# RMSNorm and matmul on one core: the first eight output tiles in one store, two loads for every later group of x, smaller last stores

## The chip, the cores and the metric

The kernel runs on one core of a Trainium2 chip. The metric is the device time in microseconds of one execution. All other times below are from one profiled execution; they count from the first instruction of the program in the profile.

## The reference

`x` has 16 x 1024 tokens of 512 features in float32, `weight` is 512 x 768, `gamma` is a vector of 512, and the output is float32.

```python
batch, seq, dim, out_dim = 16, 1024, 512, 768
def reference(x, gamma, weight, eps):
    rms = np.sqrt(np.mean(x ** 2, axis=-1, keepdims=True) + eps)
    x_norm = x / rms * gamma
    return np.matmul(x_norm, weight).astype(np.float32)
```

So 33.6 MB of x and 1.6 MB of weights are read, and 50.3 MB are written.

## The kernel before

The 16384 tokens are cut into 128 tiles of 128 tokens, one token to a partition. Two tiles make a pair `j`, and the main loop runs over the pairs. For each tile VectorE or GpSimd prepare the operand, TensorE multiplies it with the bf16 weights (gamma is multiplied into them at the start), and the row factor 1/rms is applied when the product is evicted from PSUM.

The work of one tile is this. GpSimd casts x to bf16 (`cast`, L186, or `cast_quad`, L258). Of every 16 tiles 12 are transposed by TensorE (`transpose_word`, L228) and copied out of PSUM by VectorE (`evac`, L237); the other four are transposed by VectorE alone in 32x32 blocks (`move`, L269). ScalarE sums the squares (`square`, L194), some four pairs ahead of the matmuls, takes the root (L199), and VectorE inverts it (L201). TensorE does four steps of a 512 wide and a 256 wide matmul (`product`, L298) into one of three PSUM accumulators. The eviction (`finish_tile`, through `scale`) multiplies by 1/rms and writes the tile into an output buffer: ScalarE takes the even tiles (L277), VectorE the odd ones (L279).

The buffers are counted in tiles. x has two buffers `xt` of `XG` = 16 tiles; group g of x is in buffer g % 2. The output has three buffers `ot` of `OG` = 8 tiles; group g of the output is in buffer g % 3. The helper `stretches` says in which pieces a group is moved: for x a list for the first group, `[2, 2, 4, 8]`, two halves for some groups, and otherwise the whole group; for the output likewise.

All loads of x, all weights and all stores are issued by SyncE (SP), in the order in which the program recorded them, and lie on one DMA queue. `load(i)` (L175) issues one piece of x; `store(i)` (L291) issues a piece of the output when its last tile is evicted. The two first groups of x are issued at the start, before anything else needs SP. A later group is recorded by `load_until` in the last pair of the group before the one before it, and stands on SP behind the store that ends there. So SP's order in the steady part is store, store, load, store, store, load, and each store waits for its tiles.

`rows` maps tiles to rows of x and out in HBM. Tokens are dealt so that one partition has several neighbouring tokens: in a group of 16 tiles a partition has 16 neighbouring tokens, so that a load of the whole group reads 32 KB rows, a load of a half reads 16 KB rows that are 32 KB apart, and a store of eight tiles writes 24 KB rows. The first 16 tiles are dealt by pieces: the pieces of 2, 2, 4 and 8 tiles have 2, 2, 4 and 8 neighbouring tokens to a partition, and the pieces of the output there keep to the same borders.

`Order` records every operation with the cells that it reads and writes, and `emit` works out the waits. For each engine `known` holds how far it knows every other engine and every transfer to be; `needs` are the waits that remain, and `awaited` is their union. A transfer that nobody awaited is returned in `last`, and SP waits for all of them at the end of the kernel (L468 in the profile). The last tile of a store's piece also waits for the eviction of the tile before it (`before` in `finish_tile`), so that SP needs one wait only.

Of the kernel before, what the change touches and what calls it, by code (L numbers as in the profile page):

```python
# [20 lines left out]
class Order:  # L21
# [17 lines left out]
    def emit(self):  # L39
        nc = self.tc.nc  # L40
        streams = {id(e): n for n, e in enumerate((nc.tensor, nc.vector, nc.scalar, nc.gpsimd, nc.sync))}
        writer, readers = {}, {}
        known = [dict() for _ in streams]
        clocks, needs, place, slot_of, slots = [], [], [], {}, []
        count = [0] * len(streams)
        for n, (proc, engine, _, reads, writes) in enumerate(self.ops):
            at = streams[id(engine)]
            if proc is None:
                me, turn = ("transfer", n), 1
            else:  # L50
                count[at] += 1
                me, turn = at, count[at]
            written = {writer[cell] for cell in reads + writes if cell in writer}
            read = {d for cell in writes for d in readers.get(cell, ())}
            need = []
            for d in sorted(written | read, reverse=True):
                who, when = place[d]
                if who == me and (engine is nc.tensor or d not in written):
                    continue
                if known[at].get(who, 0) < when:  # L60
                    need.append(d)
                    for k, v in clocks[d].items():
                        known[at][k] = max(known[at].get(k, 0), v)
            if proc is None:
                free = [k for k, d in enumerate(slots) if known[at].get(("transfer", d), 0)]
                if free:
                    slots[free[0]] = n
                else:
                    slots.append(n)
                slot_of[n] = ("slot", slots.index(n))  # L70
            clock = dict(known[at])
            clock[me] = turn
            place.append((me, turn))
            clocks.append(clock)
            needs.append(need)
            for cell in reads:
                readers.setdefault(cell, []).append(n)
            for cell in writes:
                writer[cell], readers[cell] = n, []
        awaited = {d for need in needs for d in need}  # L80
        last = [n for n, (me, _) in enumerate(place) if not isinstance(me, int) and n not in awaited]
        sems, marks, done = {}, {}, {}
        for n in range(len(self.ops)):
            me = slot_of.get(n, place[n][0])
            if n in slot_of or n in awaited:
                if me not in sems:
                    sems[me] = self.tc.alloc_semaphore(f"done{len(sems)}")
                done[me] = done.get(me, 0) + (16 if n in slot_of else 1)
                marks[n] = (sems[me], done[me])
        for n, (proc, engine, issue, _, _) in enumerate(self.ops):  # L90
            for d in needs[n]:
                engine.wait_ge(*marks[d])  # L92
            ins = issue()
            if n in marks:
                ins.then_inc(marks[n][0], 16 if n in slot_of else 1)
        return [marks[n] for n in last]
# [3 lines left out]
def kernel(  # L100
# [18 lines left out]
    _, O = out.shape  # L119
    K = D // P  # L120
    NT = N // P
    NP = NT // 2
    XG, OG = 16, 8
    AHEAD = 20

    def stretches(group, parts):
        first, size, i = {}, {}, 0
        for g in range(NT // group):
            for n in parts.get(g, [group]):
                for t in range(i, i + n):  # L130
                    first[t], size[t] = i, n
                i += n
        return first, size

    last = NT // OG - 1
    x_first, x_size = stretches(XG, {0: [2, 2, 4, 8], **{g: [8, 8] for g in (1, 2, 5, 6, 7)}})
    o_first, o_size = stretches(OG, {0: [2, 2, 4], 1: [4, 4], last: [4, 4]})

    def rows(ap, i, n):
        base, t = (x_first[i], x_size[i]) if i < XG else (i - i % XG, XG)  # L140
        return ap[base * P:(base + t) * P, :].rearrange("(p t) d -> p t d", t=t)[:, i - base:i - base + n, :]

    def sb(name, shape, dtype):
# [29 lines left out]
    def load(i):  # L173
        dst, to = x_of(i, x_size[i])
        order.transfer(SP, lambda: SP.dma_start(out=dst, in_=rows(x, i, x_size[i])), writes=to)  # L175
# [110 lines left out]
    def store(i):  # L286
        first, n = o_first[i], o_size[i]
        s = first // OG % 3
        if i == first + n - 1:
            src = ot[s][:, first % OG:first % OG + n, :]  # L290
            order.transfer(SP, lambda: SP.dma_start(out=rows(out, first, n), in_=src), reads=cells("ot", s, first % OG, n))  # L291
# [181 lines left out]
```

## Time and profile before

| what | value |
|---|---|
| median of 6 executions | 209.92 us (209.60 to 210.28) |
| the profiled execution | 209.96 us |
| its span, first to last instruction | 208.0 us |
| TensorE busy, granted clock | 193.2 us (93%), 0.991 |
| VectorE, ScalarE, GpSimd busy | 149.4, 144.3, 59.9 us |
| data queue (SP): bytes, share of 16 DMA engines | 85.46 MB, 97.2% |
| stores | 20: 13 of 3072 KB, 5 of 1536 KB, 2 of 768 KB |
| loads of x | 16: 11 of 2048 KB, 2 of 4096 KB, 1 of 1024 KB, 2 of 512 KB |

The span is the time between the first and the last instruction; 1.96 us of the execution's own time lie around it. A busy share is an average over the whole span. In the tables of windows a line holds the window in us, its length, the busy time and the number of instructions of TensorE, its weight loads, VectorE, ScalarE and GpSimd, then the granted clock, the mean busy share of the 16 DMA engines, and their GB/s. A packet is counted in the window in which it starts, so a short window can show a little over 1. In lines of a timeline the first two numbers are start and duration, and what stands in brackets is the idle time before and what ended it.

### The profile page before, as it was taken

The page shows a single profiled execution, that of the slowest core. Times are in us where ns is not written, and L with a number is a line of the kernel's source. Part 1 is how long each engine was busy: PE and PEld are TensorE (multiplying, and loading weights), DVE is VectorE, ACT ScalarE, POOL GpSimd, SP SyncE. Part 2 cuts the span into 40 slices and gives each one's busy share as a digit, 9 for nine tenths or more (in the row PEclk, how much of TensorE's full clock was granted, in tenths as well). Part 3 has the DMA queues.
Part 4 walks back from the last instruction along what each step waited for, and adds up shares of the span by engine and source line. Part 5 has one row for each costly group of instructions (what it writes and reads, how often), then busy time and mean ns, then how long its engine had stood idle before and what let it go on. Part 6 is the DMA issues. An engine that isn't in the chain of part 4 may idle for free.

```text
span 208.0 us, 2760 instructions
## 1 busy us (share of the span) xinstructions
PE 193.2 (93%) x1212; PEld 72.7 (35%) x717; DVE 149.4 (72%) x255; ACT 144.3 (69%) x343; POOL 59.9 (29%) x34
## 2 busy tenths in 40 slices
PE   7889999999999999997999999999999999999920
PEld 1234444333334333432334333443334333443300
DVE  0455647998499957997469984999569984999510
ACT  4698897777768496754977687677877697663310
POOL 3247642036300390004900660006700174000000
PEclk9999999999999999999999999999999999999996
DMA  6999999999999999999999999999999999996995
GB/s 228 419 447 419 353 407 432 432 438 421 447 451 428 405 424 460 417 419 424 424 424 430 421 425 433 422 427 441 416 424 432 441 441 410 444 421 255 439 392 232
DMA packets 5488, 85.62 MB, mean 412 GB/s; under 512 B 610, under 2 KB 612, under 8 KB 1380
## 3 DMA queue, kind: packets, MB, share of 16 engines
q1 hardware_dynamic: 5472, 85.46, 97.2%
q8 instruction: 7, 0.11, 0.2%
q14 instruction: 5, 0.04, 0.0%
q10 hardware_dynamic: 4, 0.00, 0.0%
HBM read 35.13 MB, written 50.33 MB: 411 GB/s over the span
## 4 chain that ended last, share of the span: by engine, by line
PE 71%; DMA 16%; DVE 5%; issue 2%; SPq 1%; ACT 1%; POOL 1%; ACTq 0%
PE ps L298 62%; DMA xt<-in_x_dram 16%; PE ps L228 8%; DVE ot L279 2%; DVE xTq L269 2%; DVE xT L237 1%; POOL xb L186 1%; ACT jk L194 0%; SPq L343 0%; SPq L175 0%; ACT ot L277 0%; SPq L291 0%; DVE rstd L201 0%; SPq L468 0%; ACTq L92 0%
## 5 line engine op out<-in xcount | busy, mean ns | idle before, releaser
L298 PE MATMUL ps<-w_bf,xT 128*128 128x256 bf16 (+1 forms) x783 | 145.0, 325 | 3.0 <-ACT ot L277 1.3
L277 ACT ACTIVATE ot<-ps,rstd 128x768 f32<-128x768 f32 x64 | 57.5, 898 | 42.6 <-PE ps L298 41.0
L194 ACT ACTIVATE jk<-xt 128x512 bf16<-128x512 f32 x128 | 78.8, 618 | 8.2 <-DMA xt<-in_x_dram 8.2
L186 POOL CAST xb<-xt 128x2048 bf16<-128x2048 f32 (+3 forms) x21 | 46.4, 2221 | 113.1 <-DMA xt<-in_x_dram 111.8
L279 DVE TENSOR_SCALAR ot<-ps,rstd 128x768 f32<-128x768 f32 x64 | 64.8, 1013 | 9.9 <-PE ps L298 9.3
L294 PEld LDWEIGHTS <-xT 128*128 128x128 bf16 x400 | 39.3, 98 | 60.8 <-issue 52.9
L228 PE MATMUL ps<-ident_f,xb 128*128 128x128 f32 x200 | 54.4, 277 | 0.9 <-POOL xb L186 0.9
L237 DVE COPY xT<-ps 128x1024 bf16<-128x1024 bf16 (+1 forms) x53 | 34.5, 653 | 24.2 <-PE ps L228 22.5
L269 DVE STREAM_TRANSPOSE xTq<-xq 32x256 f32<-32x256 f32 x112 | 48.8, 435 | 3.4
L228 PEld LDWEIGHTS ps<-ident_f,xb 128*128 128x128 f32 x200 | 28.4, 143 | 46.4 <-issue 42.9
L298 PE MATMUL ps<-w_bf,xTq 128*128 128x256 bf16 (+1 forms) x217 | 41.8, 324 | 0.4
L194 ACT ACTIVATION_READ_ACCUMULATOR jk<-xt 128x1 f32 x128 | 24.3, 190 | 0.0
L294 PEld LDWEIGHTS <-xTq 128*128 128x128 bf16 x112 | 11.0, 98 | 14.5 <-issue 14.5
L258 POOL CAST xq<-xt 128x2048 bf16<-128x2048 f32 x7 | 13.3, 1897 | 0.0
L201 DVE RECIPROCAL rstd<-rms 128x8 f32<-128x8 f32 (+3 forms) x20 | 3.9, 193 | 8.1 <-ACT rms L199 7.8
L199 ACT ACTIVATE rms<-ssq,eps_sb 128x8 f32<-128x8 f32 (+3 forms) x20 | 6.0, 300 | 0.6
L298 PE MATMUL ps<-warm 128*128 128x512 bf16 x10 | 4.4, 583 | 1.4 <-DVE eps_sb L352 1.4
L277 ACT ACTIVATE w_bf<-w_f,g_sb 128x768 bf16<-128x768 f32 x2 | 1.9, 935 | 1.3 <-DMA w_f<-in_weight_dram 1.3
L375 DVE COPY g_sb<-ps 128x4 f32<-128x4 f32 x1 | 0.2, 160 | 3.2 <-PE ps L369 3.2
L339 ACT ACT_TABLE_LOAD x1 | 1.3, 1283 | 1.5 <-SPq L432 1.5
L279 DVE TENSOR_SCALAR w_bf<-w_f,g_sb 128x512 bf16<-128x512 f32 (+2 forms) x3 | 1.4, 481 | 0.7 <-DMA w_f<-in_weight_dram 0.7
L369 PEld LDWEIGHTS ps<-ident_f,g_row 2*128 2x128 f32 x2 | 0.3, 200 | 2.6 <-issue 2.6
(10 smaller groups left out, 2.0 us busy)
## 6 DMA issues: line engine op xcount, KB each, us to landing
out_dram<-ot SPq DMA_DIRECT2D x13, 3072.0 KB, 16.0
xt<-in_x_dram SPq DMA_DIRECT2D x11, 2048.0 KB, 20.5
xt<-in_x_dram SPq DMA_DIRECT2D x2, 4096.0 KB, 23.4
out_dram<-ot SPq DMA_DIRECT2D x5, 1536.0 KB, 11.3
w_f<-in_weight_dram SPq DMA_DIRECT2D x2, 768.0 KB, 5.6
out_dram<-ot SPq DMA_DIRECT2D x2, 768.0 KB, 16.1
xt<-in_x_dram SPq DMA_DIRECT2D x2, 512.0 KB, 5.2
xt<-in_x_dram SPq DMA_DIRECT2D x1, 1024.0 KB, 9.1
```

What stands on the lines that cost most here:

```text
L186: run(POOL, lambda: POOL.tensor_copy(out=xb[s][:, i % 8:i % 8 + n, :], in_=src), of, cells("xb", s, i % 8, n))
L194: run(ACT, lambda: ACT.activation(out=jk[j], in_=src[:, 0, :], func=AF.Square, accum_out=ssq[:, i:i + 1]), of, [("jk", j), ("ssq", i)])
L199: run(ACT, lambda: ACT.activation(out=rms[:, s], in_=ssq[:, s], func=AF.Sqrt, scale=1.0 / D, bias=eps_sb), [("ssq", t) for t in range(i, i ...
L201: run(DVE, lambda: DVE.reciprocal(out=rstd[:, s], in_=rms[:, s]), [("rms", i)], [("rstd", t) for t in range(i, i + n)])
L228: run(PE, lambda: PE.transpose(out=tp[b][:, t, h, :], in_=words[:, lo:lo + P], identity=ident_f), cells("xb", s, j % 4 * 2 + t) + ["ident" ...
L237: run(DVE, lambda: DVE.tensor_copy(out=dst[:, t:t + n, :], in_=src[:, t:t + n, :]), [("tp", b)], cells("xT", j % 4, t, n))
L258: run(POOL, lambda: POOL.tensor_copy(out=xq[s], in_=src), of, [("xq", s)])
L269: run(DVE, lambda: DVE.transpose(out=dst, in_=src), [("xq", s)], [("xTq", s)])
L277: run(ACT, lambda: ACT.mul(out=dst, in_=src, mul=r), reads, writes)
L279: run(DVE, lambda: DVE.tensor_single_scalar(out=dst, in_=src, scalar=r, op=mybir.AluOpType.mult), reads, writes)
L294: run(PE, lambda: PE.ldweights(lhsT), [cell])
L298: run(PE, lambda: PE.add_instruction(mybir.InstMatmult(name=nc.get_next_instruction_name(), engine=mybir.EngineType.PE, ins=[PE.lower_ap(r ...
```

## The change

There are three edits of how the work is cut, and one in the list of final waits.

- Tiles 0 to 15 are dealt by eight tokens to a partition throughout. The loads of tiles 0-1, 2-3 and 4-7 keep their sizes, and read 4, 4 and 8 KB of every 16 KB in HBM. Output group 0 has no entry any more, so its eight tiles are stored together.
- Every group of x from 1 on is loaded in two halves; before, groups 3 and 4 were loaded whole.
- Output group 14 (tiles 112 to 119) is stored in halves, and the last group (tiles 120 to 127) in pieces of 4, 2 and 2 tiles instead of 4 and 4.
- `last` in `emit` is chosen by `known` instead of by `awaited`.

```diff
         awaited = {d for need in needs for d in need}
-        last = [n for n, (me, _) in enumerate(place) if not isinstance(me, int) and n not in awaited]
+        seen = {who for clock in known for who in clock}
+        last = [n for n, (me, _) in enumerate(place) if me not in seen and not isinstance(me, int)]
...
-    x_first, x_size = stretches(XG, {0: [2, 2, 4, 8], **{g: [8, 8] for g in (1, 2, 5, 6, 7)}})
-    o_first, o_size = stretches(OG, {0: [2, 2, 4], 1: [4, 4], last: [4, 4]})
+    x_first, x_size = stretches(XG, {0: [2, 2, 4, 8], **{g: [8, 8] for g in range(1, NT // XG)}})
+    o_first, o_size = stretches(OG, {1: [4, 4], last - 1: [4, 4], last: [4, 2, 2]})
 
     def rows(ap, i, n):
-        base, t = (x_first[i], x_size[i]) if i < XG else (i - i % XG, XG)
+        base, t = (i - i % 8, 8) if i < XG else (i - i % XG, XG)
         return ap[base * P:(base + t) * P, :].rearrange("(p t) d -> p t d", t=t)[:, i - base:i - base + n, :]
```

The order of the instructions of TensorE, VectorE, ScalarE and GpSimd stays as it is. SP has two stores fewer at the start, one load more in each of groups 3 and 4, and one store more in each of the last two output groups.

## The prediction

> **What bounds the kernel now.** I read the page first, then the DMA windows around the end, then the one stall of TensorE, then the DMA windows of the start. Two things are full at once.
>
> ```profile
> PE 193.2 (93%) x1212; PEld 72.7 (35%) x717; DVE 149.4 (72%) x255; ACT 144.3 (69%) x343; POOL 59.9 (29%) x34
> q1 hardware_dynamic: 5472, 85.46, 97.2%
> out_dram<-ot SPq DMA_DIRECT2D x1, 1536.0 KB, 6.6
> ```
>
> TensorE is busy 93% of the span, and the one data queue keeps 16 DMA engines busy 97.2% of it: 202.2 us of 208.0, with 85.46 MB. The third line is the DMA view of the last 9 us: the last store is issued at 199.98 and lands 6.6 us later, at 206.6; the span ends 1.4 us after that. Whoever stops here says: the last store is too big and too late. The windows before it say something else (window, its length, busy time of each engine, granted clock, DMA share, GB/s):
>
> ```profile
> 185.21:186.12 0.91, 0.91 (x8) 0.38 (x4) 0.88 (x4) 0.20 (x1) 0.00 (x0) 1.00 1.00 432
> 186.12:187.04 0.92, 0.92 (x8) 0.32 (x4) 0.90 (x1) 0.03 (x1) 0.00 (x0) 1.00 0.87 374
> 187.04:187.95 0.91, 0.86 (x7) 0.46 (x5) 0.87 (x2) 0.88 (x1) 0.00 (x0) 1.00 0.63 270
> 187.95:188.86 0.91, 0.91 (x8) 0.24 (x3) 0.84 (x3) 0.00 (x0) 0.00 (x0) 1.00 0.44 189
> 188.86:189.77 0.91, 0.91 (x7) 0.29 (x3) 0.88 (x2) 0.00 (x0) 0.00 (x0) 1.00 0.32 135
> 189.77:190.68 0.91, 0.91 (x8) 0.29 (x3) 0.87 (x2) 0.85 (x1) 0.00 (x0) 1.00 0.19 81
> 190.68:191.60 0.92, 0.92 (x8) 0.29 (x3) 0.86 (x2) 0.06 (x1) 0.00 (x0) 1.00 1.00 427
> ```
>
> The queue runs dry because tiles 112 to 119 are stored only at 190.23. But it does not run dry at once: the share falls step by step to 0.19, which is 3 of 16 engines, and those 3 are still at work on the old store when the new one arrives. So 13 engines idle, on average over all 16 by 0.13x0.92 + 0.37x0.91 + 0.56x0.91 + 0.68x0.91 + 0.81x0.91 = 2.33 us, and the slowest three by nothing. A transfer has landed when its last engine is done: the store issued at 177.70 lands at 192.0 (14.3 us later), some 5 us after the first engines were through. From 190.68 to the end no engine stops, and all finish together. The slowest engine is thus busy from the first load to the last store; that chain, not TensorE, sets the end.
>
> TensorE has one stall, on the load of group 4 (tiles 64 to 79), issued whole at 72.01 and landed at 96.3:
>
> ```profile
> 96.38 0.63 ACT L194 ACTIVATE jk<-xt 128x512 bf16<-128x512 f32 x1 [3.63 <-DMA xt<-in_x_dram]
> 98.55 1.46 PE L298 MATMUL ps<-w_bf,xT 128*128 128x512 bf16 x8 [1.32 <-ACT ot L277]
> ```
>
> ScalarE waits 3.63 us for the data, its eviction of tile 56 stands behind that in order, and TensorE loses 1.32 us. Last, the start:
>
> ```profile
> 22.00:24.00 2.00, 1.95 (x15) 0.84 (x9) 1.70 (x3) 1.30 (x6) 2.00 (x1) 1.00 1.12 442
> 24.00:26.00 2.00, 2.00 (x15) 0.71 (x7) 1.05 (x2) 2.00 (x6) 1.45 (x1) 1.00 0.90 213
> 26.00:28.00 2.00, 2.00 (x15) 0.82 (x9) 0.58 (x2) 2.00 (x6) 0.00 (x0) 1.00 0.96 370
> 28.00:30.00 2.00, 2.00 (x15) 0.86 (x9) 1.60 (x2) 2.00 (x7) 1.01 (x1) 1.00 0.99 413
> ```
>
> The engines stay occupied here, yet from 24 to 28 they move (427-213)x2 + (427-370)x2 = 542 KB less than at the 427 GB/s of other stretches: 1.27 us lost by all engines alike, cause not visible.
>
> **The change, part by part.** The sum is made along the slowest DMA engine, in its order of transfers, against the profiled execution: span 208.0, 1.96 around it, 209.96, which is 0.04 above the median of 209.92.
>
> *Tiles 0 to 7 in one store.* Three stores (issued 13.00, 16.51, 23.88) become one at 23.88. The early two bought nothing: the second lands 16.1 us after its issue, at 32.6, because the loads of tiles 8 to 31, 6.3 MB, were queued ahead of it and the engines are on them until about 27. The merged store is there before that, so no gap: 0. If the loads drained early, the cover would be 27 - 23.9, about 3 us. SP's later issues keep their times. Row sizes change the pace a little: 6 KB rows ran at 413 GB/s (28 to 30 us), 12 KB rows at 427 (32 to 36), 24 KB rows at 432 (184.3 to 186.1). Half of 3.146 MB at 413 and half at 427 is 7.49 us, all at 432 is 7.28: -0.21.
>
> *The first four loads, rows by eight tokens.* The loads of tiles 0-1, 2-3 and 4-7 keep rows of 4, 4 and 8 KB, now spaced 16 KB apart in HBM instead of dense. No row shows this spacing. Nearest are the 16 KB rows spaced 32 KB: 425 to 429 GB/s (40 to 46, 110.3 to 114 us) against 430 for dense 32 KB rows. Below: 0, nothing here gains from sparser rows. Above: all 2.10 MB at the worst pace seen, 213 instead of 427, is +4.9. I take 0, as the near row has the same half-skipped pattern at full pace. The Trainium skill speaks against this edit: "DMA: Bandwidth & Descriptors", Latency and other measured facts, lists copies that slow down where rows are pitched at large powers of two. Its smallest listed pitch, 512 KiB, ran at 207 GB/s beside 214 for a padded one; by that ratio, an estimate, the three loads would cost 0.2 us more, and by the trace nothing.
>
> *Groups 3 and 4 in two loads each.* Same bytes, order and issue point; one more issue on SP each (about 0.95 us), after a store and with over 9 us until SP's next: 0. Tiles 64-71 land about 2.097 MB/430 = 4.9 us before the whole, near 91.4, so the stall of 1.32 goes. TensorE then runs 1.3 us ahead. Next late are the first half of group 7 (issued 143.77, landed 165.3; by the 22.9 us that the stalled load could have taken, and 1.3 earlier, wanted at 165.4) and output buffer 2 (stored at 154.29, free at 177.5, wanted then too): both just in time. Pace: 8.389 MB at 427 instead of 430.5: +0.16. What the 1.3 us are worth at the end: nothing, since the slowest DMA engine was not waiting for TensorE.
>
> *Tiles 112-119 in two stores.* The first goes about 6 us before 190.23, while the queue is still full, so the 2.33 us of mean idle go. The slowest three had none: 0. Pace 427 for 432 on 3.146 MB: +0.09. *Last group 4, 2, 2:* the last tile is evicted near 198.6 instead of 199.95; alone, its 0.786 MB would be down by about 198.6 + 0.3 + 1.9 + 1.4, near 202, but the slowest engine still has its backlog. Pace 413 for 427 on 1.573 MB: +0.13. The skill's rule in the same page, Measured, asks for at least 1 MiB in a DMA and promises only 75% of peak from there; for these two stores, an estimate at 75% of 427, that would be 1.2 us instead of 0.13. The 6 KB rows at 413 decide. New waits of DVE on ScalarE's eviction of the tile before (tiles 115, 125) are met about a tile time earlier: 0.
>
> *"Fewer waits at the end".* A transfer enters `known` only where some engine needs it, and there it enters `awaited` too: both tests pick the same transfers. What changes is the cut of the stores: groups 13, 14, 15 leave 1+2+3 = 6 waits instead of 1+1+2 = 4. No row shows a met wait alone. Below, 0; above, the 1.4 us from the last landing to the end hold four of them and the closing barrier, so 0.35 each, 0.7. I take 0.05, because the older transfers have landed before SP looks.
>
> Sum: -0.21 + 0.16 + 0.09 + 0.13 + 0.05 = +0.22; 209.96 + 0.22 = 210.18, less 0.04: **210.1 us**. About 0.2% (0.42 us) is what can be told from no change here, so this is no change. Its own range is 209.6 to 210.7, for the engines' lags may fall a little differently.
>
> **The rivals.** *The slow stretch at 24 to 28 goes* with the transfers around it: -1.27, 208.9. For: it begins as the store at 23.88 is issued, and nothing like it with all engines comes again. Against: it hits loads that the change leaves alone, and the issues at 13.00 and 16.51 did nothing of the kind.
>
> *The end follows the mean, not the slowest engine:* if the lag of the three engines comes anew in each stretch, or they catch up when others have finished, the 2.33 us are won: 209.96 - 2.33 + 0.22, about 207.8. For: the window of 0.19, TensorE's freed 1.32. Against: three engines without any idle.
>
> *Slower: the spaced first rows.* All DMA engines carry them first, and the slowest has no slack to make it up, so each lost microsecond is one at the end. At half pace for the 1.05 MB with 4 KB of every 16 KB it is 1.05/0.213 - 1.05/0.427 = 2.5; half of that gives 211.3. It decides once tiles 4-7, landed at 11.93, come over 0.5 us later.
>
> *It doesn't do what it says:* true of the waits, and in the sum.
>
> **How the numbers follow.** No change 0.50 (in its range 0.08 faster, 0.30 same, 0.12 slower); slow stretch gone 0.16; mean engine 0.13; spaced rows 0.21. Faster 0.08 + 0.16 + 0.13 = 0.37, same 0.30, slower 0.12 + 0.21 = 0.33. The range, 208.4 to 211.4, leaves out the mean-engine case and the upper third of the spaced rows, 0.20.
>
> **What would show it.** Right: no TensorE stall at 96 to 99, DMA share at 1.0 through 186 to 191, TensorE done near 197.6, and in exchange a share that slopes down over the last 4 us with the last landing still at 206 to 207. Wrong: a square end of the DMA share near 204 (mean engine); 427 GB/s through 24 to 28; a first load landing after 4.3 and the fourth after 12.4 (spaced rows).

## The result and the profile after

The changed kernel takes 210.48 us (median of 22 runs, 210.27 to 211.54) beside 210.04 us for the kernel before in the same series (45 runs): a ratio of 1.0025, 95% interval 1.0018 to 1.0032. By the ratio it is slower by 0.53 us (by the two medians 0.44), a little over the 0.2% from which the prediction would speak of a change; the interval begins just below that. The profiled execution took 210.45 us with a span of 208.4.

The three lines of the page and of the DMA view of the end, now of the changed kernel:

```profile
PE 192.7 (92%) x1212; PEld 72.3 (35%) x717; DVE 149.3 (72%) x255; ACT 144.7 (69%) x343; POOL 60.0 (29%) x34
q1 hardware_dynamic: 5760, 85.46, 97.3%
out_dram<-ot SPq DMA_DIRECT2D x1, 768.0 KB, 7.1
```

Bytes and busy time are what they were. The last store has half the size, is issued at 199.75 instead of 199.98, and takes 7.1 us to land instead of 6.6: 206.8 instead of 206.6. The windows before the end (same columns as before: window, length, five engines, granted clock, DMA share, GB/s):

```profile
187.04:187.95 0.91, 0.86 (x7) 0.30 (x3) 0.84 (x3) 0.65 (x1) 0.00 (x0) 1.00 1.00 432
187.95:188.86 0.91, 0.91 (x7) 0.29 (x3) 0.88 (x2) 0.00 (x0) 0.00 (x0) 1.00 0.95 405
188.86:189.77 0.91, 0.91 (x8) 0.29 (x3) 0.88 (x2) 0.16 (x1) 0.00 (x0) 1.00 0.95 405
189.77:190.68 0.91, 0.91 (x8) 0.28 (x3) 0.84 (x3) 0.74 (x1) 0.00 (x0) 1.00 1.01 432
...
203.00:204.00 1.00, 0.00 (x0) 0.00 (x0) 0.00 (x0) 0.00 (x0) 0.00 (x0) 0.50 0.68 283
204.00:205.00 1.00, 0.00 (x0) 0.00 (x0) 0.00 (x0) 0.00 (x0) 0.00 (x0) 0.50 0.40 166
205.00:206.00 1.00, 0.00 (x0) 0.00 (x0) 0.00 (x0) 0.00 (x0) 0.00 (x0) 0.50 0.15 61
206.00:207.00 1.00, 0.00 (x0) 0.00 (x0) 0.00 (x0) 0.00 (x0) 0.00 (x0) 0.50 0.02 6
```

The hole of 187 to 191 is filled, as the finer store of tiles 112 to 119 was to fill it. The idle time has not gone, it has moved: after 203 one engine after another has nothing left, and from 205 on 15% of them, two or three, work for the end. The same slope stood at 187 before.

The trace says the same in another way. It has sixteen landing signals for every transfer, as many as there are engines, and a transfer has landed with the last of them. In the kernel before, those of the store issued at 177.70 come from 187.37 to 191.98, and three of them (191.72, 191.80, 191.98) only after the next store is issued at 190.23: the three engines of the share of 0.19. In the changed kernel those of the last store come from 203.29 to 206.82.

TensorE's stall at 97 is gone as well. In the timeline of the changed kernel TensorE works from 94.75 to 100 without a wait; then ScalarE, two lines of a sum of squares and the eviction that comes after them:

```profile
94.75 5.04 PE L299 MATMUL ps<-w_bf,xT 128*128 128x512 bf16 x30
97.34 0.62 ACT L195 ACTIVATE jk<-xt 128x512 bf16<-128x512 f32 x1
97.86 0.19 ACT L195 ACTIVATION_READ_ACCUMULATOR jk<-xt 128x1 f32 x1
98.53 0.90 ACT L278 ACTIVATE ot<-ps,rstd 128x768 f32<-128x768 f32 x1 [0.48 <-PE ps L299]
```

Nothing here waits for a load; ScalarE waits for TensorE. But the last eviction starts at 198.71, only 0.22 us earlier than before, because the start is late (without the late start, below, it is 1.5 us earlier). These are the first sums of squares of the kernel before and of the changed one:

```profile
4.30 0.63 ACT L194 ACTIVATE jk<-xt 128x512 bf16<-128x512 f32 x1 [1.53 <-DMA xt<-in_x_dram]
```

```profile
5.62 0.63 ACT L195 ACTIVATE jk<-xt 128x512 bf16<-128x512 f32 x1 [2.86 <-DMA xt<-in_x_dram]
```

The first load, the same 0.52 MB, is 1.32 us later. And the stretch of slow transfers has another place. First the kernel before, then the changed kernel, then its later windows:

```profile
24.00:28.00 4.00, 4.00 (x29) 1.52 (x16) 1.63 (x3) 4.00 (x11) 1.45 (x1) 1.00 0.93 291
```

```profile
24.00:28.00 4.00, 4.00 (x27) 1.57 (x16) 2.81 (x5) 3.30 (x10) 2.72 (x2) 1.00 1.02 428
...
44.00:48.00 4.00, 3.95 (x27) 1.62 (x16) 3.80 (x9) 3.08 (x9) 3.31 (x1) 1.00 1.04 336
```

At a share near 1 the engines are occupied and move a fifth to a third less: at 24 to 28 before, at 44 to 48 after (where the kernel before had 424 GB/s). The changed kernel also runs at 396 and 390 GB/s from 32 to 36 and 36 to 40.

One view would have misled here. The page's chain of waits gives 88% of the changed kernel's span to TensorE, where it gave 71% before. It is followed back from the last instruction, through the last eviction; the seven microseconds of the last store, and the queue that store stands in, are not what it counts.

### The profile page after: what moved, and what is told of

Read it like the earlier page. It is cut to its first block, busy times and chain, and to the rows that moved or that the text cites. A ratio compares the mean times of both kernels' runs of the same rounds, so it can differ in the third digit from the quotient of the medians.

```text
span 208.4 us, 2764 instructions
## 1 busy us (share of the span) xinstructions
PE 192.7 (92%) x1212; PEld 72.3 (35%) x717; DVE 149.3 (72%) x255; ACT 144.7 (69%) x343; POOL 60.0 (29%) x34
## 4 chain that ended last, share of the span: by engine, by line
PE 88%; DMA 5%; issue 1%; SPq 1%; POOL 1%; DVE 0%
PE ps L299 78%; PE ps L229 10%; DMA xt<-in_x_dram 5%; POOL xb L187 1%; DVE ot L280 0%; SPq L176 0%; SPq L344 0%; SPq L469 0%; SPq L433 0%
## 5 line engine op out<-in xcount | busy, mean ns | idle before, releaser
L299 PE MATMUL ps<-warm 128*128 128x512 bf16 x10 | 3.9, 530 | 1.4 <-DVE eps_sb L353 1.4
```

Source lines behind the costliest of these rows:

```text
L299: run(PE, lambda: PE.add_instruction(mybir.InstMatmult(name=nc.get_next_instruction_name(), engine=mybir.EngineType.PE, ins=[PE.lower_ap(r ...
```

## The experiments

Two theories ran through the prediction. By the first, the slowest DMA engine sets the end and TensorE's time does not matter; by its rival, the end follows TensorE or the mean of the engines. Medians below are beside the kernel before in the same series.

**The edits one by one.** First the halves and the finer last stores together, without the first edit:

```diff
-    x_first, x_size = stretches(XG, {0: [2, 2, 4, 8], **{g: [8, 8] for g in (1, 2, 5, 6, 7)}})
-    o_first, o_size = stretches(OG, {0: [2, 2, 4], 1: [4, 4], last: [4, 4]})
+    x_first, x_size = stretches(XG, {0: [2, 2, 4, 8], **{g: [8, 8] for g in range(1, NT // XG)}})
+    o_first, o_size = stretches(OG, {0: [2, 2, 4], 1: [4, 4], last - 1: [4, 4], last: [4, 2, 2]})
```

> The kernel before with the load halves and the finer last stores, but with tiles 0 to 7 dealt and stored as before. Slowest-engine theory (the end is the backlog of the slowest DMA engine): the first load lands at 4.3 as before, TensorE has no stall at 96 to 99 and its last eviction ends near 198.6, and still the time is 210.0 to 210.5, since only the pace terms (+0.16 +0.09 +0.13 +0.05) reach the end; the DMA share slopes down over the last 4 us. Mean-engine theory: 2.3 us are won, 207.6 to 208.0. If the late first load of the changed kernel is what made it slower, this one is at least 0.3 us faster than the changed kernel.

Measured: 210.17 beside 209.92, ratio 1.0012 (1.0001 to 1.0023). The last eviction ended at 198.4, 1.5 us before that of the kernel before, and the last store took 8.6 us to land. So 1.5 us of TensorE bought nothing. Mean-engine is out by 2 us. By the ratios it is 0.27 us faster than the changed kernel, about the 0.3 that was asked for if the late start is what makes that one slower.

Then the halves alone (the first of the two lines above):

> The kernel before with groups 3 and 4 loaded in halves and nothing else. Slowest-engine theory: TensorE's stall of 1.32 us at 97 is gone, the time is 210.04 + 0.16 = 210.2. TensorE theory (the end follows TensorE): 1.3 faster, 208.7. Third theory, halves keep the slowest engine from falling behind (its lag at 190 was 4.9 us behind the first engines before and is about 3.5 in the changed kernel): 209.0 to 209.4, with fewer windows of low DMA share before 190.7.

Measured: 209.93 beside 209.92, ratio 1.0007 (0.9992 to 1.0022). The last store was issued at 198.56 and took 7.8 us, landing at 206.3. Its windows show the next store coming sooner, which only shortens the wait of the quick engines:

```profile
187.04:187.95 0.91, 0.91 (x8) 0.29 (x3) 0.88 (x2) 0.00 (x0) 0.00 (x0) 1.00 0.63 270
187.95:188.86 0.91, 0.91 (x7) 0.29 (x3) 0.88 (x2) 0.45 (x1) 0.00 (x0) 1.00 0.44 189
188.86:189.77 0.91, 0.91 (x8) 0.24 (x3) 0.84 (x3) 0.45 (x1) 0.00 (x0) 1.00 0.95 405
```

The share falls by the same steps as before to 0.44, then the store is there, 1.4 us earlier. TensorE's theory (208.7) and the third one (209.0 to 209.4) both miss.

The finer last stores alone (`last - 1: [4, 4], last: [4, 2, 2]` in the output line):

> The kernel before with only the stores of the last two groups cut to 4, 4 and 4, 2, 2. Slowest-engine theory: the DMA share stays at 1.0 through 186 to 191, slopes down at the end, and the time is 210.04 + 0.09 + 0.13 + 0.05 = 210.3. Mean-engine theory: 210.04 - 2.33 + 0.27 = 208.0. Last-store theory (the size of the last store is what stands at the end): the last store of 0.79 MB instead of 1.57 MB saves 1.8 us, 208.2.

Measured: 210.24 beside 209.92, ratio 1.0010 (0.9991 to 1.0028). The share stayed near 1 (0.92 to 1.01) through 187 to 191, and sloped down at the end:

```profile
187.95:188.86 0.91, 0.91 (x7) 0.29 (x3) 0.85 (x3) 0.00 (x0) 0.00 (x0) 1.00 0.92 392
188.86:189.77 0.91, 0.91 (x8) 0.23 (x3) 0.90 (x1) 0.38 (x1) 0.00 (x0) 1.00 0.95 405
...
203.00:204.00 1.00, 0.00 (x0) 0.00 (x0) 0.00 (x0) 0.00 (x0) 0.00 (x0) 0.50 0.43 178
204.00:205.00 1.00, 0.00 (x0) 0.00 (x0) 0.00 (x0) 0.00 (x0) 0.00 (x0) 0.50 0.16 68
205.00:206.00 1.00, 0.00 (x0) 0.00 (x0) 0.00 (x0) 0.00 (x0) 0.00 (x0) 0.50 0.12 49
```

A last store of half the size, issued 0.45 us earlier, takes 7.6 us instead of 6.6. Neither the size of the last store nor the hole was what stood at the end.

**The first edit alone**, with the merged store (both lines) and without it (the first line):

```diff
-        base, t = (x_first[i], x_size[i]) if i < XG else (i - i % XG, XG)
+        base, t = (i - i % 8, 8) if i < XG else (i - i % XG, XG)
...
-    o_first, o_size = stretches(OG, {0: [2, 2, 4], 1: [4, 4], last: [4, 4]})
+    o_first, o_size = stretches(OG, {1: [4, 4], last: [4, 4]})
```

> The kernel before with only the first edit: tiles 0 to 7 dealt by eight tokens and stored together. Spaced-rows theory: the first load lands at 5.6 instead of 4.3 and every DMA engine carries the 1.3 us to the end, 210.04 + 1.3 - 0.21 = 211.1. Rival, absorbed: the late start is taken up by a slack that the chain has (the stall of TensorE or the 1.27 us of slow loads at 24 to 28), 209.8 to 210.2.

Measured with the merged store: 210.14 beside 209.92, ratio 1.0014 (1.0005 to 1.0023). The first load is late by the same 1.3 us, and 0.3 us arrive at the end: between the two theories, nearer to the one that says absorbed.

> The kernel before with tiles 0 to 7 dealt by eight tokens, and still stored as 2, 2 and 4 tiles. Spaced-rows theory: the first load lands at 5.6 again, the later loads take their usual time, and the time is that of the first edit with the merged store plus about 0.2 (6 and 12 KB rows instead of 24 KB). Rival, the merged store matters by itself (its early stores were of use): this one is faster than the first edit with the merged store.

Measured without the merged store: 210.12 beside 209.83, ratio 1.0017 (1.0004 to 1.0030); the first sum of squares starts at 5.57. So it is the spacing of the rows; the merged store changes nothing that can be measured. Where the slow stretch sits depends on the edit again: 44 to 48 ran at 352 GB/s with the merged store, at 409 without.

The parts add up: 0.12% for halves and last stores, 0.14% for the first edit, 0.25% for all.

**How the spacing costs.** Tiles 0 to 15 dealt by sixteen (`base, t = (i - i % XG, XG)` for all), on the changed kernel; and tiles 0 to 7 by four (`(i - i % 4, 4)`), on the kernel before:

> The changed kernel with tiles 0 to 15 dealt by sixteen tokens: the first loads read 4, 4, 8 and 16 KB of every 32 KB, so the first load touches 4 MB instead of 2 MB. If the late first load comes from how far apart its rows are, it lands later still, near 6.9 (1.3 more), and the second load over the same stretch takes its usual 1.27 us behind the weights. If it is any gap at all, it lands at 5.6 as in the changed kernel. Time: 211.5 if each microsecond at the start is one at the end, 210.5 if not.

> The kernel before with tiles 0 to 7 dealt by four tokens: the first load reads 4 KB of every 8 KB and spans 1 MB. The first load landed at 4.27 dense, at 5.6 with 16 KB between rows and at 4.96 with 32 KB. If the span that the first load touches is what costs, it lands between 4.3 and 4.9; if any gap costs, at 4.9 or later; the load of tiles 2 and 3 takes 1.26 to 1.28 us either way.

The first sums of squares of the two:

```profile
4.99 0.63 ACT L195 ACTIVATE jk<-xt 128x512 bf16<-128x512 f32 x1 [2.22 <-DMA xt<-in_x_dram]
```

```profile
5.49 0.63 ACT L194 ACTIVATE jk<-xt 128x512 bf16<-128x512 f32 x1 [2.73 <-DMA xt<-in_x_dram]
```

So the first load is late by 0.69 us with 32 KB from row to row, 1.32 with 16 KB, 1.19 with 8 KB. These differences are larger than the scatter: the first sum of squares starts at 4.19 to 4.34 in the six profiles with dense first rows, and at 5.56 to 5.67 in the five with 16 KB (8 and 32 KB have one profile each). The span that the load touches does not set the price, since the widest is the cheapest of the three; any gap costs, and not in proportion. The expectation for 32 KB was met by neither of its two cases. By sixteen took 210.24 beside 209.83, ratio 1.0028 (1.0006 to 1.0049): neither 211.5, nor clearly different from the changed kernel. Of the kernel by four there is one run, 210.74, with a profile, beside one of 210.24. In it TensorE is so late that the store of tiles 112 to 119 is issued only at 191.30, when the share has fallen to 0.06. There the last engines have run dry too, and the last signal of that store comes 7.99 us after that of the store before it, where the kernel before has 7.27. By this run a late TensorE costs nothing only as long as the slowest engine still has work.

Next the weights ahead of the first load of x, on the changed kernel:

```diff
-    load_until(2)
     load_weights(0)
     load_weights(1)
+    load_until(2)
```

> The changed kernel with both weight loads issued ahead of the load of tiles 0 and 1. Spaced-rows theory: the weights land at their usual pace (1.9 us each, the first near 6.2 less the 2.0 that the first x load took in the kernel before, so about 4.9 with the start), and the load of tiles 0 and 1 is now the late one, about 1.3 us longer than the 1.26 us of the load of tiles 2 and 3. First-transfer theory (whatever comes first is late in the changed program): the weights are late by 1.3, and the load of tiles 0 and 1 takes 1.3 us like the next.

The weights landed at 5.3 and 7.2, and the load of tiles 0 and 1 at 9.4, 2.2 us after the weights and 0.9 later than the 1.3 us that the load of tiles 2 and 3 then took. The first weights too came some 0.4 later than expected. Most of the delay goes with the spaced load, not with the place in the queue. The kernel as a whole took 214.06 us (one run, beside one of 210.24), for a reason that the prediction had named as a price: TensorE starts later, the store of tiles 0 to 7 goes out at 28.13, and the loads are through before:

```profile
25.00:27.00 2.00, 1.95 (x15) 0.89 (x9) 0.95 (x2) 2.00 (x7) 1.66 (x1) 1.00 0.70 287
27.00:29.00 2.00, 2.00 (x15) 0.85 (x9) 1.19 (x3) 1.48 (x5) 1.06 (x1) 1.00 0.17 74
```

The queue runs dry for all engines, 0.30x2 + 0.83x2 = 2.3 us on average. This is the cover of the merged store when it is gone; slower windows further on (33 to 41 at 361 GB/s) add to it.

**TensorE against the DMA engines.** Nine more matmuls of 512 columns, about 1.95 us, before tile 80, first on the changed kernel:

```diff
             a = accumulator()
+            if i == 80:
+                hold(warm[:, :P], "warm")
+                for _ in range(9):
+                    product(ops[a][:, :WIDE], warm[:, :P], warm, True, True, ["warm"], [("ops", a, 0)])
             matmuls(i, a, range(K), feed)
```

> The changed kernel with nine more 512 wide matmuls on TensorE before tile 80, about 1.95 us, whose product is overwritten. Slowest-engine theory: the last eviction ends near 201.7 instead of 199.75, and the time stays at 210.5, because the slowest DMA engine reaches the last store only at about 204.5. TensorE theory: 212.4.

Measured: 210.70 beside 209.83, five runs, ratio 1.0052 (1.0028 to 1.0075). In the profile, which is of the fastest of the five, the last store is issued 2.0 us later, at 201.77, and lands after 5.1 us at 206.8, like that of the changed kernel. The interval leaves room for 0.1 to 1 us, so it was run again where TensorE ends earlier, on the kernel with halves and finer last stores, with a control on the same chip:

> The kernel with halves and finer last stores (first tiles as before), with nine more 512 wide matmuls on TensorE before tile 80, about 1.95 us, whose product is overwritten. It has no late start, and its last eviction ended near 198.4, so after the delay it ends near 200.4. Slowest-engine theory: the ratio to the kernel before stays where it was without the delay, 1.0012 within its interval, and the last store lands near 207. TensorE theory: 1.0012 + 1.95/210 = 1.0105.

> The same kernel without the delay, on the same chip as a control: ratio 1.000 to 1.0025 to the kernel before by every theory; the difference to the delayed one is what tells: 0 to 0.3 us by the slowest-engine theory, about 2 us by the TensorE theory.

Measured: 210.19 with the delay and 210.19 without, beside 209.98; ratios 1.0014 (1.0004 to 1.0025) and 1.0011 (1.0001 to 1.0020). The last evictions of the two:

```profile
199.48 1.02 DVE L279 TENSOR_SCALAR ot<-ps,rstd 128x768 f32<-128x768 f32 x1 [1.58 <-PE ps L298]
```

```profile
197.44 1.02 DVE L279 TENSOR_SCALAR ot<-ps,rstd 128x768 f32<-128x768 f32 x1 [1.58 <-PE ps L298]
```

Two microseconds of TensorE, and no difference in the time; the last store lands at 207.1 and 206.7. This settles it: the end is not TensorE's.

Last, 1.23 us more for every DMA engine, on the changed kernel:

```diff
     load_until(2 * XG)
+    spill = sb("spill", [P, 2, D], F32)
+    order.transfer(SP, lambda: SP.dma_start(out=spill, in_=rows(x, 16, 2)), writes=["spill"])
```

> The changed kernel with one more load of 0.524 MB behind the first six loads of x, into a buffer that nobody reads. Slowest-engine theory: every DMA engine has 0.524/0.427 = 1.23 us more to do, and the time is 210.48 + 1.2 = 211.7, while TensorE is not delayed at that place. If the chain has slack (late DMA work is absorbed as the late start seems to have been), it stays within 210.4 to 210.8. TensorE theory: 210.5.

Measured: 211.03 beside 209.83, four runs, ratio 1.0058 (1.0043 to 1.0073), which is 0.7 us over the changed kernel's ratio (about 0.3 to 1.0 by the two intervals). So the time does grow with more DMA work, by less than 1.23. In this kernel the stretch of 44 to 48 is not slow:

```profile
44.00:48.00 4.00, 3.95 (x28) 1.56 (x16) 3.80 (x9) 3.09 (x9) 2.54 (x1) 1.00 1.02 434
```

Against 336 GB/s that is (434-336)x4 = 392 KB, 0.9 us at 427, given back. That would leave 0.3 of the 1.23, not 0.7. The landings of the profile show why such a sum does not come out: beside the changed kernel this one is 0.78 us late at 45 (45.34 and 44.56, the last signal of the load of tiles 32 to 39), 0.33 early one load later (50.94 and 51.27), still a little early at 170, and 0.53 late at the end (207.35 and 206.82), because its slowest engine falls back once more. That the extra work itself is what reaches the end was therefore not shown.

No version that was run beats the kernel before.

## Why the prediction was right

The likeliest case was no change at 210.1 with a small sum on the slow side (+0.22 us), and the measured time is 210.48 (+0.53), within that case's own range of 209.6 to 210.7 and on its slower edge. By the prediction's own mark of 0.2% it is even a little slower, to which the case had given 0.12 of its 0.50. The mechanism was right. That the number came so near is partly luck: one term (the spaced rows) was taken as 0, two (the merged store, the 6 KB rows) were not seen, one (the waits) was too small, and a start 1.32 us late could have cost more than the 0.3 us that it did. Point by point:

- *The slowest DMA engine sets the end.* Shown, by ruling out the others: 1.4 us less of TensorE (halves), 2 us more (the delayed pair), and the filled hole (finer last stores) all leave the time where it was, within a tenth or two of a per cent. In all fourteen profiles the last instruction ends 1.41 to 1.55 us after the last landing signal, while the time from the last eviction to that signal runs from 5.1 to 8.7 us.
- *TensorE's stall goes, worth nothing.* Both right. That TensorE would be done near 197.6 was wrong, since the late start, which the sum had at 0, ate the gain.
- *Slope for hole.* Right: share 1.0 through 187 to 191, and a slope from 203 to 206.8.
- *Pace terms and waits of the later edits,* +0.16 + 0.09 + 0.13 + 0.05 = +0.43: measured 0.12% or 0.25 us (0.02 to 0.48). The sum is of the right order, its parts are not. The 0.13 for 6 KB rows is not there: in the changed kernel the slowest engine's signals of the last stores lie 1.84 and 1.83 us apart for 0.786 MB each in 6 KB rows, and 3.72 for the 1.573 MB in 12 KB rows before them, nearly the same pace (427 and 423 GB/s). The waits, taken at 0.05, cost more: from the last signal to the last instruction it is 1.41 us in the five profiles with four stores to wait for, and 1.54 to 1.55 in the nine with six, so 0.14 for the two stores more. The Trainium skill's 1 MiB rule, "DMA: Bandwidth & Descriptors", Measured, by the prediction's estimate would have had 1.2 us for the two small stores alone; the runs exclude it for these stores, which stand in a full queue.
- *The merged store,* -0.21: not seen; with and without it the first edit costs 1.0014 and 1.0017, whose intervals overlap.
- *The spaced rows,* taken as 0 with up to +4.9: this term was mis-sized. The near row that I trusted (16 KB of every 32 KB at full pace) comes later in the run. The first load is 1.32 us late, so the sign that the rival set (first load after 4.3, tiles 4-7 after 12.4: 5.6 and 13.2) was met, and its cause was real. Its price was not: 0.3 us at the end instead of 1.2. The microsecond at the start is not simply carried on by every engine, as that rival had it. The skill's remark on rows pitched at powers of two, in the same page's Latency and other measured facts, pointed the right way, but by its ratio I had 0.2 us for three loads; here the first load alone pays 0.7 to 1.3, and the next load over the same stretch nothing that shows.
- *The slow stretch goes.* It left 24 to 28 and came back at 44 to 48, so nothing was won.
- *"Fewer waits at the end".* As read from the code, the old and the new test pick the same transfers, so this edit changes nothing, and the finer stores make SP wait at the end for six stores instead of four. No run has this edit alone.

Where the other microsecond of the late start goes can be followed by the last landing signals, here of the first edit with the merged store beside the kernel before:

| transfer | kernel before | first edit | later by |
|---|---|---|---|
| load of tiles 16 to 23 | 21.72 | 23.06 | 1.34 |
| load of tiles 24 to 31 | 28.87 | 28.91 | 0.04 |
| load of tiles 32 to 39 | 44.70 | 44.70 | 0.00 |
| load of tiles 40 to 47 | 49.92 | 51.19 | 1.27 |
| load of tiles 64 to 79 | 96.30 | 96.44 | 0.14 |
| last store | 206.62 | 206.93 | 0.31 |

At 28.9 the two are level, because the kernel before has its slow stretch there and the other has not; the stretch at 44 to 48 then puts the first edit back, and by 96 the slowest engine of the kernel before has fallen back as well. So the late start is not absorbed by waiting time: losses of the same size fall at other places in the two kernels. The quick engines stay behind by more: in the store before the hole the first signal comes 1.07 us later (188.44 and 187.37), the last one 0.38 (192.36 and 191.98). What makes single engines fall back, and what makes the slow stretches, stays open.

## What to carry to other kernels

Where a data queue is busy for the whole span, read its share in short windows (here 0.91 us) just before it runs dry: a share that falls by steps, as here, says that engines differ, and then ask which of them sets the end. Here it was the slowest, and filling the hole, splitting the last store or speeding up TensorE moved idle time about and won nothing. Test it by adding work to the engine that you believe innocent. A chain of waits that ends in an eviction can mislead: it names TensorE for 88% of the span of the kernel with halves and finer last stores too, where two microseconds more of TensorE cost nothing.

## What the hardware showed that was not expected

- The first load, 0.52 MB in 4 KB rows, takes 3.3 us from its issue to landing with dense rows, and 4.7 with rows 16 KB apart; by eight, four and sixteen tokens it is 1.32, 1.19 and 0.69 us late. The second load over the same rows keeps its 1.3 us in the changed kernel.
- All 16 engines have a stretch of four microseconds at four fifths of the pace or less, while mostly occupied, and its place goes with the order and the start of the transfers. In the six profiles with the old first tiles it is at 24 to 28 (251 to 326 GB/s); in the four with spaced rows and the merged store it is at 44 to 48 (336 to 352); with rows by eight or by four and the three early stores kept, both places are a little slow (378 to 382 and 395 to 409); with one more early load neither is. The cause is not known.
- In a queue that is kept full the engines drift apart. In the kernel before, the first and the last signal of a transfer are 0.46 us apart at 22 us, 1.8 at 29 and 4.6 at 192, and 0.5 after the hole in which the quick ones waited.
- With two more stores to wait for at the end, the time from the last landing to the last instruction is 0.14 us longer, though all but the last store had landed before.
